# A decoder layer in split fp32: where VectorE's weight sums are queued

## The chip, the cores and the metric

The kernel runs on one core of a Trainium2 chip. The metric is the device time of one execution in microseconds. The core has TensorE (PE, the matmuls), VectorE (DVE), ScalarE (ACT), GpSimd (POOL) and SyncE (SP, which here issues most of the DMAs). Each engine works through a queue of its own in the order in which instructions were put into it.

## The reference

One layer on a sequence of 512 tokens, width 2048, float32. Cut to what matters:

```python
h = rms_norm(x, g_mix); z = h @ w_in          # aq ak av rq rk rv rg
a_out = moba_attention(rot(qk_norm(aq)), rot(qk_norm(ak)), av)     # 8 heads, block-sparse
r_out = silu(rg) * group_norm(retention_chunkwise(rq, rk, rv))     # 8 heads
x = x + concat(a_out, r_out) @ w_o
h2 = rms_norm(x, g_ffn)
x = x + (silu(h2 @ w_gate) * (h2 @ w_up)) @ w_down
gate = sigmoid(rms_norm(x, g_ple) @ w_ple_gate + b_ple_gate)
x = x + (p @ w_ple_proj) * gate
```

The time is spent in the large products with w_in, w_o, w_gate and w_up (one array, w_gu), w_down (w_dn) and w_ple_gate (w_pl).

## The kernel before

**Split arithmetic.** A weight tile `raw` of 128x1024 float32 is loaded by DMA and split in two: ACT rounds it to the high part `wh` (helper line L54), DVE subtracts that from it for the low part `wl` (L55). The activations are split in the same way into factors `s` and `r`. A product is three matmuls for each 128x512 piece (L63): high by high, and the two mixed ones. TensorE needs `wh` first and `wl` second.

**Seven products for eight.** A large product is cut into quarters on both sides and done as seven products in place of eight (the scheme of Strassen and Winograd). The products are called "1", "5", "6", "3", "7", "2", "4", in this order. Their weights are a quarter of the weight ("11", "12", "21", "22") or a sum of quarters, which is built up in place: product 5 has 11 + 12, product 6 adds 22 to that, product 4 adds 21 again; product 7 has 12 + 22. These sums are DVE's 128x1024 additions `raw<-raw` (helper line L81).

**Groups and steps.** A `Group` is one block of output columns: seven products in four units, so 28 steps, each of them 12 matmuls of 128x512 on one weight tile (a few groups have three units). Sixteen of a group's 28 steps need a sum. The groups follow each other without a break in two runs: the first run (to about 345 us) ends the products of the q, k and v weights with four groups of w_vg; the last run (from about 705 us) has two groups of w_o, eleven of w_gu for SwiGLU, six of w_dn and two of w_pl. The first w_gu group, the last of w_dn and the first of w_pl get their sums ready-made from DRAM and have none on DVE. Between the runs stands attention and retention.

**Who queues what.** `run()` walks through the steps. At iteration i it writes the split of step i+2 (`extract`), the sum of step i+3 (`add`), the matmuls of step i (`multiply`), and then whatever fell due, mostly evacuations of finished products; in the last run these stand behind the `wl` of step i+1 on DVE by an issue order that the program gives (`tc.issue_after`). For all else a scheduler decides from its own estimates where an instruction stands in its engine's queue; TensorE's order is kept as written. Weights have four `raw` buffers for each of three tags and three buffers for `wh` and `wl`.

**Loads hang on these steps.** The sum of product 7 is followed by the load of quarter 21, the sum of product 4 by the load of the next group's 22, the split of product 7 by that of the next group's 12, the split of product 4 by its 11. Each is 512 KB on SP's queue:

```python
elif p == "7":
    plus(r("12"), r("12"), r("22"))
    self.load("21", u)
elif p == "4":
    plus(r("11"), r("11"), r("21"))
    self.load_next("22", u)
```

The end of the program is the evacuation of the last product: DVE rows on `v`, `e` and `y` that apply rstd, bias and the gate (L1265, L1273, L1276), and the final ones at L1228 to L1235.

Of the kernel before, what the change touches and what calls it, by code (L numbers as in the profile page):

```python
# [33 lines left out]
def layer_kernel(ctx, tc, x, xT, pT, g_mix, wqk, w_vg, qk_norm, g_ret, w_ow, g_ffn,  # L34
# [133 lines left out]
    def run(before=lambda i: None, behind=False):  # L168


        i = -3
        parts = {}
        while i < len(steps) or due:
            now[0] = i
            before(i)
            for n, act in ((2, "extract"), (3, "add"), (0, "multiply")):
                if 0 <= i + n < len(steps):
                    g, p, u = steps[i + n]
                    made = getattr(g, act)(p, u)
                    if n == 2:  # L180
                        parts[i + n] = made
            with ExitStack() as queued:
                for ins in parts.pop(i + 1, ()) if behind else ():
                    queued.enter_context(tc.issue_after(ins.ins))
                for fn in due.pop(i, []):
                    fn()
            i += 1
        steps.clear()
# [442 lines left out]
    def beside(i):  # L631
# [30 lines left out]
        if i >= 56 and i % 4 == 0 and i < 112:  # L662
            move(gu_moves.pop(0), lead[0])

    run(beside)
    s_ctx.close()
    ev_ctx.close()
# [620 lines left out]
    def before(i):  # L1288
        take_over(i)
        j, k = divmod(i - 56, 28)  # L1290
        if j >= 0 and k in (8, 11, 14, 17, 20, 23) and late:
            move(late.pop(0), lead[0])
        if i == b_at:
            load_bias()

    run(before, True)


# [69 lines left out]
```

## Time and profile before

| | us |
|---|---|
| median of 3 runs | 2336.1 (2335.06 to 2339.81) |
| the profiled execution | 2336.76, span 2335.0 |
| TensorE matmuls, busy | 2296.6 (98%) |
| DVE busy | 1926.5 (83%) |
| ACT busy | 1229.3 (53%) |
| low parts `wl` (L55), 740 | 902.2, mean 1222 ns |
| sums `raw<-raw` (L81), 348 | 420.9, mean 1223 ns |

The span is what the trace covers; the execution's own time lies 1.8 us above it. A busy share is an average over stages that have different limits, so it is to be read together with the windows of each stage. In a row of a timeline the bracket at the end tells how long the engine stood idle before it and what ended that. In a window's row stand, for each engine, the busy time and the number of instructions, then TensorE's granted clock, the share of time in which the DMA engines were busy, and what they moved.

### The profile page before, as it was taken

To read this page: it belongs to the slowest core of one execution; us is meant where nothing else is said; L and a number is where in the kernel's file an instruction comes from. 1 tells how busy PE (TensorE), PEld (TensorE's weight loads), DVE (VectorE), ACT (ScalarE), POOL (GpSimd) and SP (SyncE) were. 2 spreads that over 40 slices of the span, in tenths; PEclk is the share of its full clock that TensorE was granted. 3 is DMA by queue.
4 is the path that set the end of the run, shared out by engine and by line. 5 is a ranking of instruction groups with operands and counts; after the bars stand their busy time and mean duration, and the time that the engine had idled before them with its cause. 6 is when DMAs were issued, how large, how long until landed. Compare 5 with 4: busy or idle time off the path is not lost.

```text
span 2335.0 us, 29426 instructions
## 1 busy us (share of the span) xinstructions
PE 2296.6 (98%) x10445; PEld 1891.6 (81%) x10445; DVE 1926.5 (83%) x2601; ACT 1229.3 (53%) x1882; POOL 117.2 (5%) x135
## 2 busy tenths in 40 slices
PE   9999998999999999999999999999999999999999
PEld 7888877788887887888888888888888878888877
DVE  8887777877777987888988898889888877788798
ACT  8646444555565566545554555455445443447643
POOL 0004010100111000000000000000000000000000
PEclk9999999999999999999999999999999999999999
DMA  6635854557686789467556754775596776869863
GB/s 240 233 133 174 268 181 142 167 148 221 188 286 234 285 299 355 139 217 251 160 152 221 251 155 154 224 242 152 188 382 206 253 289 202 295 230 359 293 207 126
DMA packets 183843, 519.72 MB, mean 223 GB/s; under 512 B 20240, under 2 KB 33168, under 8 KB 179600
## 3 DMA queue, kind: packets, MB, share of 16 engines
q1 hardware_dynamic: 169600, 467.50, 56.2%
q0 software_dynamic: 13952, 50.34, 10.1%
q8 instruction: 82, 1.34, 0.2%
q14 instruction: 65, 0.53, 0.1%
q10 hardware_dynamic: 144, 0.01, 0.0%
HBM read 413.95 MB, written 149.95 MB: 242 GB/s over the span
## 4 chain that ended last, share of the span: by engine, by line
PE 53%; DVE 5%; DMA 3%; issue 1%; ACT 1%; SPq 0%; ACTq 0%; DVEq 0%
PE Y L63 23%; PE Z L63 15%; PE X L63 14%; DMA raw<-in_w_dn 2%; DVE wl L55 2%; DVE raw L81 2%; PE tp L68 1%; ACT wh L54 1%; DMA raw<-in_w_gu 0%; DMA pp<-pp 0%; DMA xin<-x 0%; DVE o L55 0%; DVE e L81 0%; DVE t L78 0%; DVE e L1273 0%
## 5 line engine op out<-in xcount | busy, mean ns | idle before, releaser
L54 ACT ACTIVATE wh<-raw 128x1024 fp32r<-128x1024 f32 (+1 forms) x740 | 782.8, 1059 | 867.2 <-PE Y L63 309.5
L55 DVE TENSOR_TENSOR wl<-raw,wh 128x1024 fp32r<-128x1024 f32 (+1 forms) x740 | 902.2, 1222 | 281.9 <-ACT wh L54 280.5
L63 PE MATMUL Y<-wh,s 128*128 128x512 f32 (+1 forms) x1704 | 537.5, 389 | 1.0 <-ACT wh L54 1.0
L81 DVE TENSOR_TENSOR raw<-raw 128x1024 f32<-128x1024 f32 x348 | 420.9, 1223 | 27.9 <-DMA raw<-in_w_vg 11.2
L63 PE MATMUL Z<-wh,s 128*128 128x512 f32 x1212 | 382.3, 389 | 0.2 <-ACT wh L54 0.2
L63 PEld LDWEIGHTS Y<-wh,s 128*128 128x128 f32 x1704 | 319.3, 188 | 66.6 <-ACT wh L54 1.4
L63 PE MATMUL Y<-wl,s 128*128 128x512 f32 x852 | 333.2, 391 | 0.8 <-DVE wl L55 0.4
L63 PE MATMUL X<-wh,s 128*128 128x512 f32 x1008 | 319.2, 390 | 3.8 <-ACT wh L54 2.1
L63 PEld LDWEIGHTS Z<-wh,s 128*128 128x128 f32 x1212 | 227.0, 188 | 46.6 <-ACT wh L54 0.7
L63 PE MATMUL Z<-wl,s 128*128 128x512 f32 (+1 forms) x606 | 238.5, 394 | 2.4 <-DVE wl L55 2.3
L63 PEld LDWEIGHTS X<-wh,s 128*128 128x128 f32 x1008 | 189.1, 188 | 43.8 <-ACT wh L54 2.5
L63 PE MATMUL X<-wl,s 128*128 128x512 f32 x504 | 197.2, 391 | 1.0 <-DVE wl L55 1.0
L63 PEld LDWEIGHTS Y<-wl,s 128*128 128x128 f32 x852 | 160.0, 188 | 36.0 <-DVE wl L55 3.3
L63 PE MATMUL Y<-wh,r 128*128 128x512 f32 x520 | 170.9, 390 | 1.3 <-ACT wh L54 1.3
L63 PE MATMUL acc<-h,wh 128*128 128x512 f32 x512 | 161.4, 396 | 0.0
L63 PEld LDWEIGHTS Z<-wl,s 128*128 128x128 f32 x606 | 113.8, 188 | 27.9 <-DVE wl L55 5.2
L63 PE MATMUL Z<-wh,r 128*128 128x512 f32 x372 | 121.9, 388 | 0.0
L63 PEld LDWEIGHTS Y<-wh,r 128*128 128x128 f32 x520 | 97.4, 188 | 22.0 <-ACT wh L54 2.2
L63 PEld LDWEIGHTS X<-wl,s 128*128 128x128 f32 x504 | 94.6, 188 | 21.6 <-DVE wl L55 2.4
L63 PEld LDWEIGHTS acc<-h,wh 128*128 128x128 f32 x512 | 91.4, 189 | 15.3 <-DVE zr L965 0.2
L63 PE MATMUL Y<-wl,r 128*128 128x512 f32 x260 | 102.3, 394 | 0.5 <-DVE wl L55 0.5
L63 PE MATMUL acc<-h,wl 128*128 128x512 f32 x256 | 100.3, 392 | 0.0
(241 smaller groups left out, 2834.7 us busy)
## 6 DMA issues: line engine op xcount, KB each, us to landing
raw<-in_w_gu SPq DMA_DIRECT2D x172, 512.0 KB, 5.8
raw<-in_w_dn SPq DMA_DIRECT2D x85, 512.0 KB, 6.2
a<-o SPq DMA_DIRECT2D x154, 256.0 KB, 4.9
raw<-in_w_vg SPq DMA_DIRECT2D x64, 512.0 KB, 5.2
s<-a SPq DMA_DIRECT2D x21, 1536.0 KB, 8.6
raw<-in_wqk SPq DMA_DIRECT2D x47, 512.0 KB, 4.8
raw<-in_w_ow SPq DMA_DIRECT2D x32, 512.0 KB, 7.1
xin<-x SPq DMA_DIRECT2D x60, 256.0 KB, 5.9
```

What stands on the lines that cost most here:

```text
L54: return (nc.scalar.activation(H, src, AF.Copy), nc.vector.tensor_tensor(L, src, H.bitcast(F32), op=ALU.subtract))
L55: nc.vector.tensor_tensor(L, src, H.bitcast(F32), op=ALU.subtract))
L63: ins = nc.tensor.matmul(*args, **kw)
L68: ins = nc.tensor.transpose(o, a, ident)
L81: nc.vector.tensor_tensor(o, a, b, op=ALU.add)
```

## The change

In `run()` the sum of step i+3 is put behind the `wl` of step i+1 on DVE, by the same `tc.issue_after` that serves the due work. It holds in both runs. Nothing is computed otherwise, and the dependencies are the same.

```diff
             for n, act in ((2, "extract"), (3, "add"), (0, "multiply")):
                 if 0 <= i + n < len(steps):
                     g, p, u = steps[i + n]
-                    made = getattr(g, act)(p, u)
+                    with ExitStack() as queued:
+                        if n == 3 and parts.get(i + 1):
+                            queued.enter_context(tc.issue_after(parts[i + 1][1].ins))
+                        made = getattr(g, act)(p, u)
                     if n == 2:
                         parts[i + n] = made
```

`parts[i + 1][1]` is the instruction that writes the `wl` of step i+1. Lines behind this place are three higher in the changed program (L1273 becomes L1276).

Before, the scheduler puts twelve of a group's sixteen sums into some nine steps around its products 1 and 5, often two or three in a row, and the four of product 4 ahead of product 2. Now one sum stands between each two `wl` rows, two steps ahead of its own.

First place: DVE at the beginning of the last w_pl group, from the `wl` of the second step of product 5. `raw_19253` and so on are the 11 quarters, `e1` an evacuated piece of the group before. Before:

```order
L55 TENSOR_TENSOR wl_19446<-raw_19271,wh_19445 128x1024
L81 TENSOR_TENSOR raw_19317<-raw_19317,raw_19127 128x1024
L81 TENSOR_TENSOR raw_19109<-raw_19109,raw_19201 128x1024
L81 TENSOR_TENSOR raw_19253<-raw_19253,raw_19157 128x1024
L81 TENSOR_TENSOR e1_19005<-e1_19005,xin_19375 128x512
L81 TENSOR_TENSOR e1_19006<-e1_19006,xin_19379 128x512
L55 TENSOR_TENSOR wl_19463<-raw_19297,wh_19462 128x1024
L81 TENSOR_TENSOR raw_19271<-raw_19271,raw_19175 128x1024
L81 TENSOR_TENSOR raw_19127<-raw_19127,raw_19219 128x1024
L55 TENSOR_TENSOR wl_19482<-raw_19317,wh_19481 128x1024
L55 TENSOR_TENSOR wl_19503<-raw_19253,wh_19502 128x1024
L81 TENSOR_TENSOR raw_19297<-raw_19297,raw_19201 128x1024
```

After, from the same `wl`:

```order
L55 TENSOR_TENSOR wl_19446<-raw_19271,wh_19445 128x1024
L81 TENSOR_TENSOR raw_19317<-raw_19317,raw_19127 128x1024
L81 TENSOR_TENSOR e1_19006<-e1_19006,xin_19379 128x512
L55 TENSOR_TENSOR wl_19463<-raw_19297,wh_19462 128x1024
L81 TENSOR_TENSOR raw_19253<-raw_19253,raw_19157 128x1024
L55 TENSOR_TENSOR wl_19482<-raw_19317,wh_19481 128x1024
L81 TENSOR_TENSOR raw_19271<-raw_19271,raw_19175 128x1024
L55 TENSOR_TENSOR wl_19503<-raw_19253,wh_19502 128x1024
L81 TENSOR_TENSOR raw_19297<-raw_19297,raw_19201 128x1024
L55 TENSOR_TENSOR wl_19520<-raw_19271,wh_19519 128x1024
```

Before, three and two sums stood in one piece between two `wl` rows; now there is one between each two.

Second place: DVE at the end of the program, from the `wl` of the last unit of product 2 on; `wl_19841`, `wl_19858` and `wl_19875` are those of product 4. Before:

```order
L55 TENSOR_TENSOR wl_19808<-raw_19697,wh_19807 128x1024
L1273 SCALAR_TENSOR_TENSOR e5_19555<-e5_19555,rstd2_85,bias_19019 128x512
L1265 SCALAR_TENSOR_TENSOR e1_19498<-e1_19498,minus_6586,bias_19017 128x512
L1273 SCALAR_TENSOR_TENSOR e5_19556<-e5_19556,rstd2_85,bias_19019 128x512
L1265 SCALAR_TENSOR_TENSOR e1_19499<-e1_19499,minus_6586,bias_19017 128x512
L55 TENSOR_TENSOR wl_19841<-raw_19253,wh_19840 128x1024
L1276 TENSOR_TENSOR e5_19555<-e5_19555,pp_19772 128x512
L55 TENSOR_TENSOR wl_19858<-raw_19271,wh_19857 128x1024
L1276 TENSOR_TENSOR e5_19556<-e5_19556,pp_19776 128x512
L81 TENSOR_TENSOR e5_19555<-e5_19555,xin_19771 128x512
L55 TENSOR_TENSOR wl_19875<-raw_19297,wh_19874 128x1024
```

After, from the same `wl`:

```order
L55 TENSOR_TENSOR wl_19808<-raw_19697,wh_19807 128x1024
L81 TENSOR_TENSOR raw_19271<-raw_19271,raw_19651 128x1024
L81 TENSOR_TENSOR e5_19555<-e5_19555,e1_19498 128x512
L81 TENSOR_TENSOR e5_19556<-e5_19556,e1_19499 128x512
L55 TENSOR_TENSOR wl_19841<-raw_19253,wh_19840 128x1024
L81 TENSOR_TENSOR raw_19297<-raw_19297,raw_19670 128x1024
L1276 SCALAR_TENSOR_TENSOR e5_19555<-e5_19555,rstd2_85,bias_19019 128x512
L1268 SCALAR_TENSOR_TENSOR e1_19498<-e1_19498,minus_6586,bias_19017 128x512
L1276 SCALAR_TENSOR_TENSOR e5_19556<-e5_19556,rstd2_85,bias_19019 128x512
L1268 SCALAR_TENSOR_TENSOR e1_19499<-e1_19499,minus_6586,bias_19017 128x512
L55 TENSOR_TENSOR wl_19858<-raw_19271,wh_19857 128x1024
L81 TENSOR_TENSOR raw_19317<-raw_19317,raw_19697 128x1024
```

Before, the four sums of product 4 stood ahead of these rows, among the `wl` rows of products 3 and 7. Now the first stands one `wl` ahead of these rows, and the other three, of `raw_19271`, `raw_19297` and `raw_19317`, in them.

At the end of the first run, in the same way, the four sums of product 4 of the last w_vg group now stand among the rows with which DVE prepares attention (the rotary tables `rope`, L775 and L778, and the mean squares `ms`, L845 and L846).

Third place: SP's queue where SwiGLU passes to w_dn. `raw_14941` of in_w_gu is the last load of 21, and the other `raw_149..` are loads of 12 for w_dn; `raw_15032`, `15059`, `15080` are loads of 22, `raw_15056` and `15077` of 11; `s` and `r` are factors of the activations. Before:

```order
L287 DMA raw_14961<-in_w_dn 128x1024
L243 DMA s7_15009<-a0_7_104 128x3072
L287 DMA raw_15032<-in_w_dn 128x1024
L287 DMA raw_15059<-in_w_dn 128x1024
L243 DMA r7_15010<-a0_7_104 128x1024
L287 DMA raw_15080<-in_w_dn 128x1024
L287 DMA raw_15103<-in_w_dn 128x1024
L287 DMA raw_15056<-in_w_dn 128x1024
L243 DMA s2_15094<-a0_2_105 128x3072
L287 DMA raw_15077<-in_w_dn 128x1024
L243 DMA r2_15095<-a0_2_105 128x1024
```

After, from the second load of 12:

```order
L290 DMA raw_14915<-in_w_dn 128x1024
L290 DMA raw_14941<-in_w_gu 128x1024
L290 DMA raw_14938<-in_w_dn 128x1024
L290 DMA raw_14961<-in_w_dn 128x1024
L246 DMA s7_15009<-a0_7_104 128x3072
L246 DMA r7_15010<-a0_7_104 128x1024
L290 DMA raw_15032<-in_w_dn 128x1024
L290 DMA raw_15059<-in_w_dn 128x1024
L246 DMA s2_15094<-a0_2_105 128x3072
L290 DMA raw_15056<-in_w_dn 128x1024
L290 DMA raw_15080<-in_w_dn 128x1024
L246 DMA r2_15095<-a0_2_105 128x1024
```

Before, all loads of 21 preceded those of 12, and all of 22 those of 11; now the last load of 21 stands among those of 12, and the first load of 11 ahead of the third of 22. The same holds at every passage from group to group.

## The prediction

> **What bounds the kernel now.** I read the page's busy shares first, then its groups, then windows by stage, the chain of waits, and last the timelines where TensorE stands still.
>
> ```profile
> PE 2296.6 (98%) x10445; PEld 1891.6 (81%) x10445; DVE 1926.5 (83%) x2601; ACT 1229.3 (53%) x1882; POOL 117.2 (5%) x135
> L55 DVE TENSOR_TENSOR wl<-raw,wh 128x1024 fp32r<-128x1024 f32 (+1 forms) x740 | 902.2, 1222 | 281.9 <-ACT wh L54 280.5
> L81 DVE TENSOR_TENSOR raw<-raw 128x1024 f32<-128x1024 f32 x348 | 420.9, 1223 | 27.9 <-DMA raw<-in_w_vg 11.2
> ```
>
> TensorE is the bound: 98% of 2335.0 us, so everything the change can win lies in the 38.4 us (2335.0 − 2296.6) that it stands still, whereas it can lose anywhere. DVE, at 83%, is the second. The moved sums are the x348 of 1223 ns. The windows say where the 38.4 us are, in two answers set one behind the other:
>
> ```profile
> core 0: us, PE busy (x) PEld busy (x) DVE busy (x) ACT busy (x) POOL busy (x), PEclk, DMA share, GB/s
> 30.00:340.00 310.00, 307.60 (x1350) 252.39 (x1349) 251.67 (x282) 170.51 (x274) 34.57 (x23) 1.00 0.58 191
> 340.00:400.00 60.00, 52.24 (x231) 41.85 (x230) 48.59 (x103) 30.89 (x59) 5.35 (x4) 0.94 0.52 171
> 705.00:870.00 165.00, 160.96 (x746) 132.00 (x745) 142.88 (x193) 94.02 (x163) 5.02 (x6) 1.00 0.73 264
> 870.00:900.00 30.00, 27.60 (x132) 22.06 (x131) 25.48 (x50) 22.44 (x47) 1.01 (x1) 1.00 1.03 415
> 900.00:1735.00 835.00, 834.87 (x3758) 690.64 (x3757) 706.86 (x841) 421.94 (x553) 38.09 (x56) 1.00 0.65 208
> 1735.00:2165.00 430.00, 427.00 (x1899) 350.52 (x1898) 356.09 (x403) 202.53 (x257) 0.00 (x0) 1.00 0.75 265
> 2165.00:2300.00 135.00, 133.02 (x596) 108.97 (x595) 114.74 (x154) 75.82 (x109) 1.03 (x1) 1.00 0.67 226
> ...
> 1700.00:1745.00 45.00, 45.00 (x202) 37.27 (x201) 34.95 (x38) 18.30 (x21) 0.00 (x0) 1.00 1.03 414
> 1860.00:1905.00 45.00, 44.05 (x193) 35.81 (x192) 33.74 (x36) 16.88 (x16) 0.00 (x0) 1.00 1.02 398
> ```
>
> In the eleven SwiGLU groups (900 to 1735) TensorE misses 0.13 us in 835. Nothing can be won there.
>
> **The unit prices.** Sums that stand back to back, as three in 3.50 us and two in 2.37 us below, start (3.50 − 2.37) = 1.13 us apart; that is what one costs the rows behind it. A stall costs more than its idle row. In the next fence a 128x512 matmul lasts 0.39 but the next starts 0.23 later, and the first behind a wait is 0.50: so (0.39 − 0.23) + (0.50 − 0.39) = 0.27 on top of each.
>
> **Part 1, the hoisted sums go: gains.** The front matter's first place is the beginning of the last group. The DVE rows there (2263 to 2273), then TensorE's:
>
> ```profile
> 2263.16 3.50 DVE L81 TENSOR_TENSOR raw<-raw 128x1024 f32<-128x1024 f32 x3
> ...
> 2267.77 1.23 DVE L55 TENSOR_TENSOR wl<-raw,wh 128x1024 fp32r<-128x1024 f32 x1
> 2268.91 2.37 DVE L81 TENSOR_TENSOR raw<-raw 128x1024 f32<-128x1024 f32 x2
> ...
> 2267.89 0.73 PE L63 MATMUL Y<-wh,r 128*128 128x512 f32 x2 [1.17 <-ACT wh L54]
> 2269.06 0.50 PE L63 MATMUL Z<-wl,s 128*128 128x512 f32 x1 [0.44 <-DVE wl L55]
> ...
> 2269.86 0.39 PE L63 MATMUL Z<-wl,s 128*128 128x512 f32 x1
> 2270.09 0.39 PE L63 MATMUL Z<-wh,s 128*128 128x512 f32 x1
> ```
>
> Three sums stand ahead of one wl and two of the next. With one sum ahead of each wl, five fewer stand in front of this place by the order, 5 × 1.13 = 5.7 us, more than is missing: the 1.98 us of 2165 to 2300, in three waits, go: 1.98 + 3 × 0.27 = **−2.8**.
>
> In the first run (30 to 340) the 2.40 us are six waits on a wl behind a hoisted sum: 2.40 + 6 × 0.27 = **−4.0**. The cause is seen at the fifth of them:
>
> ```profile
> 322.39 1.23 DVE L81 TENSOR_TENSOR raw<-raw 128x1024 f32<-128x1024 f32 x1 [3.22 <-DMA raw<-in_w_vg]
> ...
> 324.81 0.50 PE L63 MATMUL Z<-wl,r 128*128 128x512 f32 x1 [0.54 <-DVE wl L55]
> ```
>
> A sum for product 4 was issued before its load had landed, and the wl behind it stood for 3.22 us. Later sums find the data there. In w_dn (1735 to 2165) 3.00 us in five waits are 3.00 + 5 × 0.27 = 4.35; about 2.4 of that lies in the stretch 1860 to 1905, where the DMA engines are full (0.95 idle in its row, and more just behind). The rest, **−2.0**, is behind hoisted sums and goes. In w_o (705 to 870) most of the 4.04 us waits for attention. Two waits are on weights, and these go:
>
> ```profile
> PE Y L63 <- DVE wl L55: 0.5, 1, 0.5
> PE Y L63 <- ACT wh L54: 0.2, 1, 0.2
> ```
>
> 0.5 + 0.2 + 2 × 0.27 = **−1.2**. SwiGLU **−0.1**, the 0.13 us above.
>
> **Part 2, the four sums of product 4 go late: losses.** Before, they ran ahead of product 2, where DVE has idle time; now each stands behind the wl one row before its own product, beside the evacuations of products 7 and 2. Inside a row of groups the next group hides that (DVE waits for ACT in 281.9 us of the page's wl row). Where a row of groups ends, there is no such cover:
>
> At the program's end, the second place. Three kinds of DVE row, and one of TensorE's:
>
> ```profile
> 2285.97 1.23 DVE L81 TENSOR_TENSOR raw<-raw 128x1024 f32<-128x1024 f32 x1 [0.86 <-DMA raw<-in_w_pl]
> ...
> 2308.36 1.23 DVE L55 TENSOR_TENSOR wl<-raw,wh 128x1024 fp32r<-128x1024 f32 x1 [0.81 <-ACT wh L54]
> ...
> 2322.82 1.23 DVE L55 TENSOR_TENSOR wl<-raw,wh 128x1024 fp32r<-128x1024 f32 x1
> ...
> 2326.51 0.75 DVE L1228 SCALAR_TENSOR_TENSOR e<-Y,rstd,e 128x512 f32<-128x512 f32 x1
> ...
> 2326.42 0.28 PE L63 MATMUL Y<-wl,s 128*128 128x256 f32 x1
> ```
>
> From 2308.36 to the first row of the final evacuation at 2326.51 no DVE row waits. All four sums move from 2285.97 to 2296.9 into this stretch: 4 × 1.13 = **+4.5** on the last evacuation and so on the end. The lower bound is TensorE's own: the last wl of 1024 comes three sums, 3.4 us, later by the order, and it had 2326.42 − (2322.82 + 1.23) = 2.4 to spare: +1. I take the upper one, since this DVE stretch has no idle row into which a sum could fall.
>
> At the end of the first run four sums likewise enter the block of rope and mean-square rows ahead of attention:
>
> ```profile
> 345.68 0.69 DVE L775 TENSOR_TENSOR rope<-cs,sides 128x512 f32<-128x512 f32 x1 [0.77 <-DMA cs<-in_rope_c]
> ...
> 347.95 1.21 DVE L55 TENSOR_TENSOR wl<-raw,wh 128x1024 fp32r<-128x1024 f32 x1
> 349.22 0.66 PE L63 MATMUL X<-wl,h 128*128 128x512 f32 x1 [1.81 <-DVE wl L55]
> 349.69 1.05 PE L63 MATMUL X<-wh,h 128*128 128x512 f32 x2
> ...
> 350.00:353.00 3.00, 3.00 (x9) 2.28 (x9) 3.00 (x5) 0.69 (x1) 1.95 (x2) 0.53 0.92 283
> ```
>
> DVE is late already (TensorE waited 1.81 us for that wl). Four sums more are 4.5 us, less the 0.8 that DVE waits in that block for a table: +3.7 at most, and 0 if attention has room for it. I take **+3.1**, near the upper end: attention starts from DVE's rows, and 340 to 400, where TensorE misses 7.76 us, has a TensorE that waits for them.
>
> A row of its own for the clock: in 350 to 353 the granted clock is 0.53, and two matmuls take 1.05 (0.23 + 0.39 = 0.62 at full clock), after a gap of 1.81 us. If this gap goes, some 1.8 us of slow matmuls (nine, each 0.2 too long) go as well; if it grows, they stay. I count none of it.
>
> [...]
>
> Between w_o and SwiGLU (870 to 900) DVE has 25.48 of 30 us and the DMA engines are full (1.03). The last wl's before it had some 0.5 to 1 us to spare, and get 1.7 to 3 us later by the sums counted ahead of them: between 0 and +3, I take **+2.2**.
>
> **Part 3, the loads.** The sum of product 7 issues the load of quarter 21, the sum of product 4 the next group's 22. Both move with their sums on SP's queue: they no longer precede the loads of 12 and 11 but alternate with them, two of 512 KB in a step, where before it was one. A step is 12 matmuls of 0.227 = 2.72 us, so 1.05 MB in 2.72 us is 385 GB/s. Third place, SwiGLU to w_dn, ACT's rows:
>
> ```profile
> 1734.09 1.06 ACT L54 ACTIVATE wh<-raw 128x1024 fp32r<-128x1024 f32 x1 [1.77 <-DMA raw<-in_w_dn]
> 1739.09 1.06 ACT L54 ACTIVATE wh<-raw 128x1024 fp32r<-128x1024 f32 x1 [3.94 <-DMA raw<-in_w_dn]
> ```
>
> The engines are full there (1.03, 414 GB/s) and the split waits for the landing. A load of 512 KB is 0.524 / 0.414 = 1.27 us of all engines; those now begun some 7 us later fall into full time. One to two loads late: 1.3 to 2.5, less what margin there is (0.1 to 0.2): **+2.0**, bounds 0 and +5 (four loads). The same from w_dn's first to its second pair (1.02, 398 GB/s): **+1.5**, and before its third **+1.0**, both reckoned from the first.
>
> Within SwiGLU I cost the alternation at nothing. What hides it is this slack at a handoff, of the first 11 load of a group, issued 1256.37:
>
> ```profile
> raw<-in_w_gu SPq DMA_DIRECT2D x1, 512.0 KB, 8.4
> ...
> 1266.00 1.23 DVE L55 TENSOR_TENSOR wl<-raw,wh 128x1024 fp32r<-128x1024 f32 x1 [1.49 <-ACT wh L54]
> ...
> 1271.09 0.39 PE L63 MATMUL X<-wl,s 128*128 128x512 f32 x1
> ...
> 1249.00:1257.00 8.00, 8.00 (x38) 6.60 (x36) 5.99 (x7) 3.44 (x4) 0.83 (x1) 1.00 0.97 275
> ```
>
> The wl ends at 1267.23 and is used at 1271.09: 3.86 us. The load may take 8.4 + 3.86 = 12.3 us. Two 22 loads newly next to it are 2.5 us, 10.9 in all: hidden, with 1.4 to spare.
>
> **The sum.** Gains −4.0 −1.2 −0.1 −2.0 −2.8 = −10.1. Losses +3.1 +2.2 +2.0 +1.5 +1.0 +4.5 = +14.3. Together **+4.2**. The profiled execution took 2336.8 us and would take 2341.0; it stands 0.7 over the median 2336.1, and on that median the time is 2340.3, **2340** rounded. 0.2% is 4.7 us, about what a measurement of this kernel can tell from no change; +4.2 lies just inside.
>
> **The rivals.**
> B, faster: the gains stay and only the end is paid, since the handoffs' losses (+3.1, +2.2, +2.0, +1.5, +1.0) are estimates from margins. −10.1 + 4.5 = −5.6, 2330.5. It decides if the first run's four sums don't delay attention (3.1) and the loads land in time (2.0 + 1.5 + 1.0 = 4.5). For it: the gains are waits that stand in rows, those losses do not. Against: the full DMA windows. 0.17.
> C, slower: the load bursts make the first 11 load of each SwiGLU group late. It decides once landing takes over 12.3 us. For it: the engines are already at 0.97 in 1249 to 1257, and at 275 GB/s there, so two loads may cost 2 × 0.524 / 0.275 = 3.8 us, 12.2. One microsecond beyond at ten handoffs is +10 on my sum: 2350. Against: DMA share over all of 900 to 1735 is 0.65. 0.25.
> D, no change: gains and losses cancel, or the scheduler's order hides both: 2336. 0.13.
>
> [...]
>
> **How the numbers follow.** My forecast has 0.45: of it 0.27 within 4.7 us, 0.18 above. Faster 0.17 (B); same 0.27 + 0.13 = 0.40; slower 0.18 + 0.25 = 0.43. The range reaches from just above B's centre, 2331, to just below C's, 2349. My forecast's own is 2336 to 2345: the clock's −1.8 and 2.2 from attention's room at one end, the w_dn bound (+5 for +2.0) and that of w_o to SwiGLU (+3 for +2.2) at the other.
>
> **What would show it.** Right: no wait of a raw sum for in_w_vg above 1 us; TensorE's rows of 2258 to 2273 without a wait; the first row of the final evacuation some 4.5 us later against TensorE's last matmuls, with a sum between each of the last wl's; a longer wait of wh for in_w_dn at 1735. Wrong: TensorE missing more than 1 us in the SwiGLU windows (then C), or 340 to 400 as short of busy time as the first run got faster (then B). I would be wrong most easily in the load times, which no row of before shows at this rate.

## The result, and the profile after

The changed kernel takes 2357.65 us (median of 4 runs, 2355.56 to 2359.24), the kernel before 2337.78 on the same count: 1.0085 times as long, 95% interval 1.0068 to 1.0103, or 20 us. Forecast were 2340 and a range that ended at 2349. The profiled execution has a span of 2354.9 us against 2335.0.

The page after, the same lines as before:

```profile
PE 2306.8 (98%) x10445; PEld 1897.8 (81%) x10445; DVE 1920.9 (82%) x2601; ACT 1232.1 (52%) x1882; POOL 117.5 (5%) x135
L55 DVE TENSOR_TENSOR wl<-raw,wh 128x1024 fp32r<-128x1024 f32 (+1 forms) x740 | 901.8, 1220 | 318.1 <-ACT wh L54 314.3
L81 DVE TENSOR_TENSOR raw<-raw 128x1024 f32<-128x1024 f32 x348 | 423.9, 1218 | 0.0
```

The sums no longer wait for any load (27.9 us before, 0.0 now), and one takes 1218 ns (1223 before). The low parts wait longer for ACT's high parts: 314.3 us where it was 280.5.

To see where, I matched the two traces, of one execution each, by the k-th matmul on a `wl` into X, Y or Z, of which both have 2816, and took the difference of the start times at the stages' ends. The loss is the growth of that difference; times are those of before. "Alone" is a run below that has the new queueing in that stage only.

| stage, us | forecast | whole change | alone |
|---|---|---|---|
| first run, to 331 | −4.0 | −5.0 | −4.1 (e1) |
| end of it, attention, to 708 | +3.1 | +4.0 | +2.7 (e1) |
| w_o, to 865 | −1.2 | −2.5 | −2.2 (e2) |
| passage to SwiGLU, to 899 | +2.2 | +4.7 | +5.6 (e2) |
| SwiGLU, to 1734 | −0.1 | +9.9 | +9.2 (e3) |
| passage to w_dn, to 1798 | +2.0 | +2.0 | +2.4 (e3) |
| w_dn first pair, to 1895 | −2.0 | −1.3 | −1.2 (e4) |
| passage to the second pair, to 1925 | +1.5 | +5.1 | +2.5 (e4) |
| rest of w_dn and first w_pl group, to 2253 | +1.0 | +1.8 | +1.6 (e4) |
| last group, to 2297 | −2.8 | −3.2 | |
| end | +4.5 | +4.4 | |

The whole change adds up to 19.9, the difference of the spans. Windows of the changed kernel, columns as before:

```profile
30.00:340.00 310.00, 310.00 (x1369) 256.72 (x1368) 252.25 (x284) 173.94 (x281) 19.90 (x23) 1.00 0.59 195
...
870.00:900.00 30.00, 25.78 (x109) 20.05 (x108) 21.72 (x43) 19.61 (x40) 1.01 (x1) 0.89 1.03 410
900.00:1735.00 835.00, 829.15 (x3717) 683.03 (x3716) 693.16 (x834) 420.49 (x549) 38.19 (x56) 1.00 0.62 201
...
2165.00:2300.00 135.00, 135.00 (x613) 111.88 (x612) 114.06 (x160) 79.80 (x121) 1.03 (x1) 1.00 0.73 253
```

The first run and the last group have no idle TensorE left, as forecast (307.60 and 133.02 before). SwiGLU, which had missed 0.13 us in 835, misses 5.85 now. What happens there is read from ACT's timeline in one of three groups that stall, then DVE's and TensorE's at the same place:

```profile
1304.68 0.42 ACT L54 ACTIVATE o<-t 128x256 fp32r<-128x256 f32 x1
...
1306.44 0.42 ACT L54 ACTIVATE o<-t 128x256 fp32r<-128x256 f32 x1 [0.38 <-ACT wh L54]
1307.10 0.75 ACT L54 ACTIVATE o<-t 128x256 fp32r<-128x256 f32 x2 [0.25 <-DVE t L78]
1311.98 0.42 ACT L54 ACTIVATE o<-A 128x256 fp32r<-128x256 f32 x1 [4.13 <-DMA a<-o]
1312.31 1.04 ACT L54 ACTIVATE wh<-raw 128x1024 fp32r<-128x1024 f32 x1
...
1304.79 1.23 DVE L55 TENSOR_TENSOR wl<-raw,wh 128x1024 fp32r<-128x1024 f32 x1 [0.19 <-ACT wh L54]
...
1306.27 0.41 DVE L55 TENSOR_TENSOR o<-t,o 128x256 fp32r<-128x256 f32 x1
...
1313.40 0.73 PE L63 MATMUL Z<-wh,s 128*128 128x512 f32 x2 [1.08 <-ACT wh L54]
1314.66 0.50 PE L63 MATMUL Z<-wl,s 128*128 128x512 f32 x1 [0.53 <-DVE wl L55]
```

`o` is a tile into which a finished SwiGLU block is split as factors for w_dn (seven for a block, twice), before SP stores it to DRAM (`a<-o`). ACT writes its high part, DVE its low part, and there are four buffers. ACT has four `o` in a row between two `wh`: at 1306.44, two from 1307.10 on, and the fourth at 1311.98. The fourth needs the buffer of the `o` of 1304.68. DVE made the low part of that one at 1306.27, behind a `wl`; SP issued the store at 1306.71, and it landed at 1311.90, 5.2 us later. ACT stands 4.13 us, and the next `wh`, for which TensorE waits, stands behind it.

Before, ACT's `o` rows at this place had a `wh` between them:

```profile
1305.90 0.71 ACT L54 ACTIVATE o<-t 128x256 fp32r<-128x256 f32 x2
1307.71 1.06 ACT L54 ACTIVATE wh<-raw 128x1024 fp32r<-128x1024 f32 x1 [1.10 <-PE Z L63]
1309.66 0.42 ACT L54 ACTIVATE o<-t 128x256 fp32r<-128x256 f32 x1 [0.89 <-DMA a<-o]
1311.60 0.42 ACT L54 ACTIVATE o<-t 128x256 fp32r<-128x256 f32 x1 [1.52 <-DMA a<-o]
```

Over SwiGLU the kernel before never has more than three `o` between two `wh`; the changed one has four in nine groups. So the scheduler's order on ACT is new, although the change gives an order for DVE's rows alone. Neither half of the way to a free buffer got longer on the mean over the 140 `o`: DVE's low part begins 1.48 us behind the end of ACT's high part (1.52 before), and a store lands 3.3 us after its issue (4.7 before). In the three groups that stall, the store in question lands 5.0 to 5.2 us after its issue, in the other six 2.9 to 4.5 us, and some 8 us ahead of the stall ACT had already stood 3.3 to 4.3 us for another store (3.44 at 1303.43), without a gap on TensorE. Why the stores are late in these three stays open.

The chain of waits over SwiGLU has this row, before and after:

```profile
ACT o L54 <- DMA a<-o: 23.2, 26, 1.7
```

```profile
ACT o L54 <- DMA a<-o: 41.5, 21, 4.2
```

Such a wait was there before, but 1.7 us at most. The end of the program went as forecast (DVE, then TensorE):

```profile
2325.05 1.22 DVE L81 TENSOR_TENSOR raw<-raw 128x1024 f32<-128x1024 f32 x1
...
2336.91 1.22 DVE L81 TENSOR_TENSOR raw<-raw 128x1024 f32<-128x1024 f32 x1
...
2346.45 0.75 DVE L1231 SCALAR_TENSOR_TENSOR e<-Y,rstd,e 128x512 f32<-128x512 f32 x1
...
2342.98 0.50 PE L63 MATMUL Y<-wl,s 128*128 128x512 f32 x1 [1.46 <-DVE wl L55]
```

Four sums, the first at 2325.05 and the fourth at 2336.91, and no DVE row between them and the final evacuation waits.

### The profile page after: what moved, and what is told of

It is laid out like the page before. It is cut to its first block, busy times and chain, and to the rows that moved or that the text cites. A ratio compares the mean times of both kernels' runs of the same rounds, so it can differ in the third digit from the quotient of the medians.

```text
span 2354.9 us, 29459 instructions
## 1 busy us (share of the span) xinstructions
PE 2306.8 (98%) x10445; PEld 1897.8 (81%) x10445; DVE 1920.9 (82%) x2601; ACT 1232.1 (52%) x1882; POOL 117.5 (5%) x135
## 4 chain that ended last, share of the span: by engine, by line
PE 79%; DMA 8%; DVE 8%; issue 2%; ACT 2%; POOL 1%; SPq 0%; ACTq 0%; DVEq 0%; POOLq 0%
PE Y L63 29%; PE Z L63 20%; PE X L63 18%; PE acc L63 8%; PE at L63 2%; DMA a<-o 2%; DVE wl L55 2%; PE tp L68 2%; DMA raw<-in_w_dn 2%; DVE raw L81 2%; POOL rs L84 1%; ACT wh L54 1%; DMA s<-a 1%; DMA raw<-in_w_gu 1%; DMA mix<-o 1%
## 5 line engine op out<-in xcount | busy, mean ns | idle before, releaser
L55 DVE TENSOR_TENSOR wl<-raw,wh 128x1024 fp32r<-128x1024 f32 (+1 forms) x740 | 901.8, 1220 | 318.1 <-ACT wh L54 314.3
L81 DVE TENSOR_TENSOR raw<-raw 128x1024 f32<-128x1024 f32 x348 | 423.9, 1218 | 0.0
L63 PEld LDWEIGHTS Y<-wh,r 128*128 128x128 f32 x520 | 97.5, 188 | 19.9
```

What stands on the lines that cost most here:

```text
L55: nc.vector.tensor_tensor(L, src, H.bitcast(F32), op=ALU.subtract))
L63: ins = nc.tensor.matmul(*args, **kw)
L81: nc.vector.tensor_tensor(o, a, b, op=ALU.add)
```

## The experiments

Each run was compared with the kernel before on its own chip. Single executions of that unchanged kernel lay between 2330 and 2351 us, so the ratios say little below 0.15%; the places come from the matched traces. There too a stage with unchanged code differs between executions: by −0.7 to +7.2 us in the first run, by −1.7 to +1.8 at the passage to SwiGLU, and by up to 2 us elsewhere.

**Each stage alone** (e1 to e4). The edit is a condition on the step whose sum it is:

```diff
-                        if n == 3 and parts.get(i + 1):
+                        if n == 3 and parts.get(i + 1) and not behind:                      # e1
+                        if n == 3 and parts.get(i + 1) and behind and i + 3 < 56:           # e2
+                        if n == 3 and parts.get(i + 1) and behind and 56 <= i + 3 < 364:    # e3
+                        if n == 3 and parts.get(i + 1) and behind and 364 <= i + 3 < 518:   # e4
```

> The new queueing in the first run alone (the four w_vg groups); w_o, SwiGLU, w_dn and w_pl as before. Matching the two traces matmul by matmul put the changed kernel 5.0 us ahead at the end of the first run and 1.0 ahead at the start of w_o. Theory (attention takes the gain back, because the four sums of product 4 stand in the rows that prepare it): TensorE 4.5 to 5 us ahead at the end of the first run, 1 ahead at w_o, 1 us faster in all. Rival (the give-back comes from elsewhere, such as where the other DMAs happened to fall): 3 to 5 us faster in all.

Measured: ratio 0.999 (0.9973 to 1.0006). TensorE is 4.1 us ahead at 331 and 1.4 at 708, close to the theory's 4.5 to 5 and 1; the ratio can't tell 1 us from 3 to 5. Executions with an unchanged first run lose −1.8 to +4.5 between 331 and 708, so the give-back in attention isn't shown to be the sums' doing.

> The new queueing in the two w_o groups alone. Theory (each stage's loss belongs to the sums of that stage): w_o gains 2.5 us, the passage to SwiGLU loses 5.2, together 2.7 slower, all of it before 900 us, and TensorE without a gap from there to 1735. Rival (the lateness at the passage shifts stores and loads and so makes the stalls later in SwiGLU): another 3 to 9 us between 1300 and 1640.

Measured: 1.0009 (0.9995 to 1.0023). −2.2 within w_o, +5.6 at the passage, and 0.9 from there to 1734: the theory holds, the passage belongs to w_o's own sums and SwiGLU doesn't inherit it.

> The new queueing in the SwiGLU groups alone. Theory (in SwiGLU the sums change where ScalarE's rounding of the new factors o stands, and that waits for the stores of the buffers it reuses, with the next wh behind it): waits of ACT o for DMA a<-o of about 4 us, stalls of TensorE of 2 to 4 us in some groups, together 9, and 2 to 3 more at the passage to w_dn whose loads these sums issue: 11 to 12 slower. Rival (SwiGLU inherits the trouble from w_o's end): no stall in SwiGLU, 0 to 3 slower.

Measured: 1.0047 (1.0031 to 1.0063), 11.0 us. The same three groups stall, with ACT waits for `a<-o` of 3.4 and 4.0, 4.8 and 4.0, 3.4 and 4.0 us; +9.2, and +2.4 at the passage to w_dn. The theory holds.

> The new queueing in the w_dn groups alone. Theory (loads of 21 and 22 issued late collide with those of 11 and with the factors at the passages): 1.7 us won behind hoisted sums, 6 to 7 lost at the first matmuls of the two later pairs, about 4.5 to 5 slower. Rival (the lateness of the SwiGLU passage is what makes w_dn's waits): within 1 us of before, or faster by the 2 us of the hoisted sums.

Measured: 1.0015 (0.9996 to 1.0034). −1.2 in the first pair, +2.5 and +1.6 at the passages: 2.9 net, less than the theory's 4.5, so about half of the whole change's +5.1 at 1900 is w_dn's own.

**By product** (e5, e6): `and p != "4"`, and `and p == "4"`, in the same line.

> The new queueing in all groups, but only for the sums of products 5, 6 and 7; those of product 4 are left to the scheduler as before. Theory (the late sums of product 4, and the loads of 22 behind them, make the losses where a row of groups ends): no loss before w_o, at the passage to SwiGLU, at the passages of w_dn and at the end of the program; the gains of the first run, w_o, w_dn and the last group stay (4 + 2 + 2 + 3 = 11 us), and so do the stalls within SwiGLU (10 us), since those stand beside the sums of product 7: within 3 us of before. Rival (the sums of product 7, with their loads of 21, make the passages late): still 5 us lost at the passage to SwiGLU and 5 in w_dn, 8 to 10 slower than before.

Measured: 1.0116 (1.01 to 1.0133), 27 us, worse than the whole change. Both theories missed. The passage to SwiGLU loses 2.6 us, and SwiGLU 22.5. ACT's waits for `a<-o` are there too, of up to 4.5 us. Besides, the scheduler now puts product 4's sums among those of product 7 (DVE, then TensorE):

```profile
1487.12 1.22 DVE L81 TENSOR_TENSOR raw<-raw 128x1024 f32<-128x1024 f32 x1
1489.36 1.23 DVE L81 TENSOR_TENSOR raw<-raw 128x1024 f32<-128x1024 f32 x1 [1.02 <-DMA raw<-in_w_gu]
1490.51 1.22 DVE L55 TENSOR_TENSOR wl<-raw,wh 128x1024 fp32r<-128x1024 f32 x1
1491.64 2.35 DVE L81 TENSOR_TENSOR raw<-raw 128x1024 f32<-128x1024 f32 x2
...
1491.78 0.50 PE L63 MATMUL Y<-wl,s 128*128 128x512 f32 x1 [1.10 <-DVE wl L55]
```

Two sums stand ahead of one `wl`, the second waits for its load, and TensorE waits for that `wl`: the fault of before, at another place. The parts are not additive, since what is left free moves too.

> The complement: the new queueing in all groups for the sums of product 4 alone. Theory: 3 to 4 us at the start of attention, 5 at the passage to SwiGLU, 2 at that to w_dn, 2 to 5 within w_dn, 4.5 at the end, and no stall in SwiGLU: 14 to 18 slower. Rival (product 7's loads): losses at the end only, 4 to 6 slower.

Measured: 1.0096 (1.0075 to 1.0117), 22 us; the profiled execution, the fastest of four, ends 17.7 after before's. By the matched traces +2.1 between 331 and 708 (the theory had 3 to 4), +2.8 in w_o, +2.7 at the passage to SwiGLU, +0.9 in SwiGLU, −0.3 at that to w_dn, +2.7 and +2.8 within w_dn, +4.4 at the end. SwiGLU and the end are as the theory has them. The passage to SwiGLU takes half of its loss from product 4's sums, and that to w_dn none.

**The o buffers** (e7, e8, e10, e12). e7 and e8 space the two sets of factors, e7 with the new queueing in SwiGLU alone, e8 without it:

```diff
-                    later(1 + 2 * u, lambda u=u, sink=sink: to_factors(lambda b: act[b], 2 * u, sink))
+                    later(1 + 6 * u, lambda u=u, sink=sink: to_factors(lambda b: act[b], 2 * u, sink))
```

> The new queueing in the SwiGLU groups alone, as once before, and the second of the two sets of new factors of each group is made and stored six steps later than the first where it was two. Theory (four buffers for o, and fourteen stores in a few steps, so that ScalarE waits for a store with wh behind it): the three stalls of 10 us in all fall below 2 us, the 2 to 3 us at the passage to w_dn stay: 2 to 5 slower than before. Rival (the stalls come from late loads or from VectorE's share, and the waits for the stores are beside the point): still 8 us or more between 1300 and 1640.

Measured: 1.0063 (1.0042 to 1.0085); SwiGLU loses 11.2. But ACT's rows show the same four `o` in a row between two `wh`, with waits up to 4.7 us: the edit didn't take the pressure away, and the run decides nothing.

> Control: the kernel before with the second set of factors six steps later in the same way and nothing else changed. All theories: TensorE has no gap in SwiGLU before, so nothing can be won there; within 2 us of before.

Measured: 1.0011 (0.9997 to 1.0025), −0.4 in SwiGLU, as expected.

e10 gives the factors more room, with the new queueing in SwiGLU alone; e12 does so in the whole change:

```diff
-                    sink = spill(s_a[kg], 2 * (j - 4 * kg) + u)
+                    sink = spill(s_a[kg], 2 * (j - 4 * kg) + u, other=lambda shape: ev_tile("g", 4, shape, dt=F32R))
```

`other` takes three of a set's seven factors ("5", "3" and "2") to the buffers of tag g.

> The new queueing in the SwiGLU groups alone, with three of each set of seven factors in the four buffers of g, so that o's four buffers serve four factors of a set. The spacing of the run e7_swiglu_spaced had left ScalarE's order as it was, with four o in a row between two wh, and so did not test this. Theory (ScalarE waits for a store that frees an o, with wh behind it): the waits of 3 to 4 us for a<-o go, the 10 us between 1300 and 1640 fall below 2; the 2 us at the passage to w_dn stay. Rival (the o wait is beside the point): 8 us or more remain between 1300 and 1640.

Measured: 0.9996 (0.9982 to 1.001). The windows of SwiGLU, e3 and then e10:

```profile
900.00:1735.00 835.00, 828.64 (x3721) 682.02 (x3720) 694.31 (x834) 421.37 (x553) 38.09 (x56) 1.00 0.62 202
```

```profile
900.00:1735.00 835.00, 835.00 (x3763) 691.02 (x3762) 703.42 (x843) 426.33 (x559) 38.11 (x56) 1.00 0.63 208
```

TensorE misses nothing in this stretch, and of ACT's waits for `a<-o` none is left (in e12 one of 0.9 us); the 2.4 us at the passage to w_dn are gone too (0.0), which the theory had kept. ACT's order differs too, as the scheduler sees other buffers: four factors in a row still stand between two `wh` in ten groups, but two of them are in g's buffers. Stores of `o` land up to 7.9 us after their issue (10.1 in the kernel before). So neither four rows in a row nor a late store costs anything by itself; shown is that the wait for a buffer makes the loss, and that room for the factors takes it away.

> The whole change, with three of each seven SwiGLU factors in g's buffers. Theory (the o buffers carry SwiGLU's loss, and with them SP's stores the 2 us at the passage to w_dn): nothing lost between 900 and 1800, so 10 to 12 us less than the changed kernel: 8 to 10 slower than before. Rival (in the whole change SwiGLU's loss has another cause): 15 or more slower.

Measured: 1.0025 (1.0009 to 1.004), 5.8 us in place of 20; 0.2 us lost from 899 to 1734 and −0.9 to 1798. Better than the theory by 2 to 4.

**Late loads** (e9): the kernel before, with only the loads that the sums set off made to wait.

```diff
+            if pace[0] is not None:
+                paced(ins, pace[0])
             self.raw[q, u] = t
...
+                    pace[0] = parts[i + 1][1] if n == 3 and parts.get(i + 1) else None
                     made = getattr(g, act)(p, u)
+                    pace[0] = None
```

> The kernel before, with its sums where they were on VectorE, but every load that a sum sets off (21 and the next group's 22) waits for the wl behind which the changed kernel queues that sum; SP's queue then has the changed kernel's order. Theory (late loads make the losses where w_o passes to SwiGLU, SwiGLU to w_dn, and within w_dn): 3 to 5 us lost between 865 and 900, about 2 at 1740, 2 to 5 at 1900, 2 at 2070, none within SwiGLU (no change of the sums there) and none at the end; 8 to 12 slower, also with the gains absent. Rival (VectorE's and ScalarE's rows make those losses, the loads land early enough either way): under 2 us at each of these places.

Measured: 1.0091 (1.007 to 1.0112), 21 us, but not where the theory put it: −0.1 at the passage to SwiGLU and +0.6 at that to w_dn; +2.5 at 1900 as in e4, and +2.6 behind it (1.6 in e4). The rest is mostly a gap of 4.8 us that ends at 353 and 9.5 us in SwiGLU, where ACT waits for `a<-o` up to 5.3 us and DVE's sums of product 4 stand later by the pacing. So late loads of 21 and 22 can make half of the whole change's +5.1 at the first passage within w_dn and its +1.8 behind that, and neither of the other two passages. The sums of product 4 stand later in w_dn as well, so the run doesn't part the loads from the sums; but ACT's waits from 1895 to 1930, before and e9, are for loads:

```profile
ACT wh L54 <- DMA raw<-in_w_dn: 1.5, 1, 1.5
```

```profile
ACT wh L54 <- DMA raw<-in_w_dn: 12.9, 4, 5.2
```

**The passage from w_o** (e13): `and behind and i + 3 < 56 and p in "56"`.

> The new queueing in the w_o groups alone and only for the sums of products 5 and 6. Theory (the sums of 7 and 4 make the splits of these products late, and these set off the loads of 12 and 11, which then stand on SP behind the reloads of s): no loss at the passage, TensorE between 865 and 900 within 1.5 us of before; the gain of 2 us within w_o falls to between 0 and 2. Rival (the later evacuations on VectorE, not the loads, make the passage late): 3 us or more lost between 865 and 900.

Measured: 1.005 (1.0029 to 1.007), 12 us. The profiled execution, the slowest of seven, ends 19.5 after before's, and 9.6 of that were there at 708, ahead of every changed step. +1.5 at the passage, which is just what the theory allows and no more than unchanged executions show. +5.0 within w_o: 2.9 up to 730, where attention's last matmuls stand (one waits 2.1 us for DVE), and 2.1 from 800 on, where TensorE waits for `wl`. ACT also waits 4.6 us for a store of h (`h<-o`, the same kind of wait), but TensorE loses nothing there. With e5 and e6, the run speaks for the sums of 7 and 4. ACT's `wh` wait for loads of in_w_gu at the passage: 4.4 us in the changed kernel, 5.3 in e2, 3.5 here, 2.1 in e9 and 1.7 before. What makes these loads late stays open.

**A version where it pays** (e11): the new queueing in the first run and for the last group, whose product 4 sums are issued nine steps ahead.

```diff
-            for n, act in ((2, "extract"), (3, "add"), (0, "multiply")):
+            for n, act in ((2, "extract"), (3, "add"), (9, "add"), (0, "multiply")):
                 if 0 <= i + n < len(steps):
                     g, p, u = steps[i + n]
+                    tail = behind and i + n >= 546 and p == "4"
+                    if act == "add" and n != (9 if tail else 3):
+                        continue
...
+                        if act == "add" and (not behind or i + n >= 546) and parts.get(i + 1):
+                            queued.enter_context(tc.issue_after(parts[i + 1][1].ins))
```

> The new queueing only where the runs so far show a gain: the first run, and products 5, 6 and 7 of the last w_pl group; there the sums of product 4 are issued nine steps ahead in place of three, so that they stay out of the last rows. All else as before. Theory: 3 to 4 us from the first run, 2.8 from the last group, up to 1 given back by the order of the last evacuations: 4 to 6 faster (ratio 0.9975 to 0.9983). Rival (attention and the end take it all back): within 2 us.

Measured: 0.9982 (0.9966 to 0.9999), some 4 us faster than before and 24 than the change. Its span is 2331.9. Its windows:

```profile
2165.00:2300.00 135.00, 135.00 (x609) 111.87 (x609) 114.84 (x153) 75.76 (x108) 1.03 (x1) 1.00 0.67 229
30.00:340.00 310.00, 310.00 (x1369) 256.76 (x1369) 252.01 (x283) 174.44 (x280) 19.92 (x23) 1.00 0.58 194
```

Both gains are there: −4.2 at 331 and −3.1 in the last group. Not all of it is kept: TensorE is level with before at 865 (+0.1), a give-back within what unchanged executions show, and the end still costs 2.4 us, 1.0 of them up to TensorE's last matmuls, where up to 1 was expected.

## Why the prediction was wrong

- The sign of the sum was right, the size was not: +4.2 forecast, 19.9 measured. Most of the 15.7 us is one step: "Within SwiGLU I cost the alternation at nothing" (Part 3; −0.1 in the sum), where the whole change lost 9.9. The slack that I named there, of the first load of 11, held: e10 and e12 issue the loads in the changed kernel's order and lose nothing. I had looked at DVE and SP, and not at ACT's queue, on which the new order on DVE brought four `o` in a row; the fourth waits for the store that frees its buffer, and `wh` stands behind it. With more buffers the loss is gone (e10, e12). The row to start from stood in the waits of before (23.2 us for `a<-o`, 26 times).
- Rival C had SwiGLU as the place (+10 there) and the wrong cause: bursts of loads. Its time, 2350, was 8 us short as well.
- "Between w_o and SwiGLU … between 0 and +3, I take +2.2": 4.7, and 5.6 alone. The bound was wrong, as it counted late `wl` only; what the rows show is `wh` late behind loads of in_w_gu (4.4 us, 1.7 before). Late loads of 21 and 22 don't make it (e9), and its cause stays open.
- The passage to w_dn's second pair, +1.5 "reckoned from the first": 5.1. With the new queueing in w_dn alone it is 2.5, and with late loads alone 2.5 too, so the cause was right for half of it, and the other half stays open. That to the first, +2.0, measured as forecast by luck. `wh` did wait longer for in_w_dn there (12.5 us from 1730 to 1800, 10.2 before), but with more o buffers and the same queueing it waits 8.4 (e12) and the loss is gone, so the loads' alternation doesn't make it by itself.
- Right: the first run's −4.0 (−5.0, −4.1 alone), the last group's −2.8 (−3.2), w_dn's hoisted sums −2.0 (−1.3), w_o's −1.2 in sign (−2.5), and the end's +4.5 (+4.4, of which 2.4 up to TensorE's last matmul and 2.0 on DVE behind it). The give-back in attention, +3.1, measured +4.0, but unchanged runs scatter as much.

## What to carry to other kernels

When instructions move in one engine's queue and a scheduler orders the rest, look at the new order of the other engines too, and count the tiles written in a row against their buffers and the stores that free them. A wait that is short and covered in the profile of before (1.7 us for a store in this case) can grow (to 4.2) and stand in front of what the busiest engine needs. Match two traces by the same instruction and read the loss by stage: a sum of right terms with a zero in it can still be far off. An order that helps where the weight sums bunch should be given there alone, and its late part kept out of the end, where no next group covers it.

## What the runs showed of the hardware

After short gaps TensorE's clock was low in some places and full in others. In the changed kernel's SwiGLU:

```profile
1395.10 0.84 PE L63 MATMUL Z<-wh,s 128*128 128x512 f32 x2 [1.87 <-ACT wh L54]
...
1396.96 1.05 PE L63 MATMUL Z<-wh,s 128*128 128x512 f32 x2
...
1399.05 0.62 PE L63 MATMUL Z<-wh,s 128*128 128x512 f32 x2
```

Behind a gap of 1.87 us two matmuls take 1.05 us at 1396.96, where two take 0.62 at 1399.05; the granted clock is 0.50 over 1396.90 to 1399.00. Behind one of 1.08 at 1313.40 they take 0.73, and the granted clock is 1.00 over 1310 to 1320. The kernel before kept a granted clock of 1.00 over 870 to 900 with a gap of 2.07 in it, where the changed one, with two such gaps of 3.5 us together (1.85 the longer), has 0.89. So a gap of 2.07 us stands without a lower clock and one of 1.87 with it: the length of a gap alone doesn't tell which follows, and what else does isn't shown here.
